# Attention of the first layer: three passes on full-array tiles against plain fp32 on half-array tiles

## The chip, the cores and the metric

The kernel runs on one core of a Trainium2 chip. The metric is the device time of one execution in microseconds (us); the figure quoted for a kernel is the median of its runs. The core has TensorE (PE; its weight loads are PEld), VectorE (DVE), ScalarE (ACT), GpSimd (POOL) and SyncE (SP), each working through its own queue in order.

## The reference, cut to what matters

Four layers work on 128 context tokens and 512 latent tokens, 1024 features each. Layer 0's token mixer is attention with 16 query heads and 4 key/value heads of 64 features: the context tokens attend to themselves, the latent tokens to a band of three blocks of 128 keys around their own block and to 128 cached context keys. Every head has a sink in its softmax.

```python
q, k, v = split_qkv(h, wqkv)          # latent: q, k rotated by position
s_loc = where(|kpos - qpos| <= 128 and 0 <= kpos < T, q . kb * 64 ** -0.5, -1e30)
s_ctx = q . ck * 64 ** -0.5
p = softmax(concat([s_loc, s_ctx, sink]))
o = p_loc @ vb + p_ctx @ cv           # then o @ wo
x = x + gate * (o @ wo)               # then the gated ConvFFN, and layers 1 to 3
```

## The kernel before

Features lie on the partitions and all 640 tokens on the free axis. A projection of full precision is made in three passes: weights and activations are split into a high part (a rounding to fp32r) and a low part (the rest), and `mm3` adds high x high, high x low and low x high. A weight tile of 128 outputs takes 48 matmuls of 320 columns (eight k steps, two halves, three passes). `Weights` loads the tiles in order of their use and splits them (`pump1`: the high part on ScalarE, the low one on VectorE or GpSimd). How far ahead it may go is set by `slots` and `cap`. `Ada` works out the modulation vectors of later layers in quarters of a row block (`micro`) as fillers, on VectorE or on GpSimd followed by a sum on ScalarE. `filler(rate)` gives four quarters times the rate.

The order on every engine is the order in which the program is written; nothing reorders it. In layer 0's mixer the projections come in the order k0, k1, q0, v0, v1, q1 to q7, the first three as a leading group. Attention then goes through 40 units of two heads each: a prompt unit has 128 keys, a latent unit 384 or 512. Query heads are kept in pairs (e = 0 and 1, on partitions 0 to 63 and 64 to 127). Keys of one e are kept with the other 64 partitions zero, so that a score uses the full array. The stages of a unit are

- `scores`: three passes of q x k per head into a PSUM pair, a bf16 mask added by a product with the identity, then on VectorE the maximum over keys (L777) and the bias (L779);
- `exps`: the sink's difference (L784), two exponentials on ScalarE out of PSUM (L786), the sink's exponential (L788);
- `scale`: sum, reciprocal and division of P by it, one head on VectorE (L795), one on GpSimd (L796);
- `transp`: P's blocks of 128 keys transposed on TensorE (L805);
- `evac_hi`, `evac_lo`: P out of PSUM, high part on ScalarE (L811), low part on VectorE (L817);
- `pv`: three passes with V for both heads (L450 to L452 by `mm3`), and every second unit a split of the result into the input of the output projection.

They are a pipeline over units: step u holds the scores and exponentials of unit u, the scaling of u - 1, transposes and copies of u - 2 and the V products of u - 3. Units 0 to 2 are called from `post` of the last query tiles, the others from a loop. The output projection's eight tiles follow (two of them begin during the last steps).

## Time and profile before

| | us |
|---|---|
| median of 3 runs | 2775.72 |
| lowest to highest | 2769.52 to 2777.26 |
| span of the profiled execution | 2775.9 |

The profiled execution lies at the median. TensorE's busy time includes modelled ends of matmuls, which overlap the next one; the pace of a stream is read from the distance between starts. The stages of the first mixer are read from the start: projections, units, output projection.

### The profile page before, as it was taken

Reading aid. Unit: us, or ns where it says so; the run is one execution under the profiler, and the core shown is the slowest. Engines: PE = TensorE matmul, PEld = TensorE weight load, DVE = VectorE, ACT = ScalarE, POOL = GpSimd, SP = SyncE. Lnnn points to the kernel's source line nnn. Section 1 sums busy time; section 2 is a strip of 40 time slices with the busy share of each in tenths; the row PEclk is TensorE's granted clock in tenths of the full one; section 3 lists DMA queues with packets and bytes.
Section 4 is the critical chain, followed back from the end, with each engine's and each line's share of the span. In section 5 each row is a group of like instructions: output and inputs, shape, how many; then the busy total and the mean of one; then the engine's idle time right before and its main releaser. Section 6 shows DMA issues by size and latency. Waiting matters only on the chain.

```text
span 2775.9 us, 45101 instructions
## 1 busy us (share of the span) xinstructions
PE 2706.1 (97%) x18494; PEld 2655.7 (96%) x18494; DVE 1873.1 (67%) x2851; ACT 1097.3 (40%) x1832; POOL 976.9 (35%) x517
## 2 busy tenths in 40 slices
PE   8888999999999999999999999999999999999998
PEld 6776999999999999999999999999999999999998
DVE  5889888695964459586886435968778649534344
ACT  4467454343433235333444222533434425323232
POOL 1555154453620027344542001644354215212121
PEclk9999999999999999999999999999999999999999
DMA  6311434343422225343432222434343124222221
GB/s 245 103 31 39 145 108 135 131 145 129 147 74 70 84 62 171 121 141 118 157 102 74 84 76 70 152 116 151 112 153 135 46 69 138 75 78 69 84 70 45
DMA packets 87489, 295.34 MB, mean 106 GB/s; under 512 B 9585, under 2 KB 15345, under 8 KB 87281
## 3 DMA queue, kind: packets, MB, share of 16 engines
q1 hardware_dynamic: 86706, 292.19, 31.8%
q8 instruction: 146, 2.39, 0.3%
q14 instruction: 61, 0.50, 0.1%
q10 hardware_dynamic: 576, 0.26, 0.0%
HBM read 289.53 MB, written 2.88 MB: 105 GB/s over the span
## 4 chain that ended last, share of the span: by engine, by line
PE 85%; DVE 8%; issue 4%; ACT 1%; POOL 1%; DMA 0%; SPq 0%; POOLq 0%; DVEq 0%; ACTq 0%
PE up L452 15%; PE up L450 15%; PE up L451 15%; PE dn L452 6%; PE dn L450 6%; PE dn L451 6%; PE sc L451 2%; PE sc L452 2%; PE sc L450 2%; DVE t L378 1%; DVE asm L777 1%; DVE asm L784 1%; PE sv L450 1%; PE sv L451 1%; PE sv L452 1%
## 5 line engine op out<-in xcount | busy, mean ns | idle before, releaser
L451 PE MATMUL up<-h,w 128*128 128x320 f32 x2816 | 872.6, 310 | 1.7 <-DVE h L390 1.7
L450 PE MATMUL up<-h,w 128*128 128x320 f32 x2816 | 873.5, 310 | 0.0
L452 PE MATMUL up<-h,w 128*128 128x320 f32 x2816 | 872.1, 310 | 0.0
L86 DVE TENSOR_TENSOR w<-raw,w 128x1024 fp32r<-128x1024 f32 (+1 forms) x269 | 476.4, 1773 | 102.0 <-ACT w L85 94.6
L451 PEld LDWEIGHTS up<-h,w 128*128 128x128 f32 x2816 | 530.4, 188 | 3.1 <-DVE h L390 2.8
L450 PEld LDWEIGHTS up<-h,w 128*128 128x128 f32 x2816 | 530.4, 188 | 0.3
L452 PEld LDWEIGHTS up<-h,w 128*128 128x128 f32 x2816 | 530.4, 188 | 0.0
L212 POOL TENSOR_TENSOR adaq<-adaq,cb 128x1024 f32<-128x1024 f32 x145 | 366.4, 2527 | 370.5 <-ACT adaq L213 321.5
L86 POOL TENSOR_TENSOR w<-raw,w 128x1024 fp32r<-128x1024 f32 (+1 forms) x87 | 211.6, 2433 | 761.8 <-ACT w L85 635.2
L85 ACT CAST w<-raw 128x1024 fp32r<-128x1024 f32 (+1 forms) x356 | 363.3, 1022 | 242.8 <-PE dn L452 163.0
L450 PE MATMUL dn<-g,w 128*128 128x320 f32 x1408 | 436.4, 310 | 0.0
L451 PE MATMUL dn<-g,w 128*128 128x320 f32 x1408 | 435.1, 309 | 0.0
L452 PE MATMUL dn<-g,w 128*128 128x320 f32 x1408 | 435.1, 309 | 0.0
L573 ACT ACTIVATE c<-up,fcv 128x640 f32<-128x640 f32 x176 | 139.9, 795 | 607.9 <-PE up L452 604.0
L575 DVE SCALAR_TENSOR_TENSOR c<-up,fcv,c 128x127 f32<-128x127 f32 x352 | 191.4, 544 | 213.4 <-ACT c L573 213.4
L207 DVE CUSTOM_DVE_ANT_0 adaq<-adaq,cb 128x1024 f32<-128x1024 f32 x145 | 272.6, 1880 | 0.1
L542 DVE SCALAR_TENSOR_TENSOR x<-dn,mod,x 128x128 f32<-128x128 f32 (+3 forms) x204 | 99.4, 527 | 251.0 <-PE dn L452 250.9
L451 PEld LDWEIGHTS dn<-g,w 128*128 128x128 f32 x1408 | 264.3, 188 | 0.3
L450 PEld LDWEIGHTS dn<-g,w 128*128 128x128 f32 x1408 | 264.3, 188 | 0.3
L452 PEld LDWEIGHTS dn<-g,w 128*128 128x128 f32 x1408 | 264.3, 188 | 0.0
L597 POOL TENSOR_TENSOR c<-c,c 128x640 f32<-128x640 f32 x64 | 154.4, 2412 | 158.4 <-DVE c L577 158.4
L577 DVE SCALAR_TENSOR_TENSOR c<-up,fcv,c 128x127 f32<-128x127 f32 x352 | 193.6, 550 | 12.4
(234 smaller groups left out, 4371.5 us busy)
## 6 DMA issues: line engine op xcount, KB each, us to landing
raw<-up SPq DMA_DIRECT2D x176, 512.0 KB, 4.3
adaq<-ada_t SPq DMA_DIRECT2D x145, 512.0 KB, 3.6
raw<-down SPq DMA_DIRECT2D x64, 448.0 KB, 3.5
raw<-down SPq DMA_DIRECT2D x32, 512.0 KB, 3.9
ada<-ada_t SPq DMA_DIRECT2D x31, 512.0 KB, 3.5
raw<-sc_in SPq DMA_DIRECT2D x24, 512.0 KB, 3.5
ada<-ada SPq DMA_DIRECT2D x16, 512.0 KB, 10.2
raw<-sgu_in SPq DMA_DIRECT2D x16, 512.0 KB, 3.5
```

The costliest lines, as they stand in the source:

```text
L85: nc.scalar.copy(w[:, 0, :n], raw[:, :n])
L86: (nc.gpsimd if pool else nc.vector).tensor_tensor(out=w[:, 1, :n], in0=raw[:, :n], in1=w[:, 0, :n], op=ALU.subtract)
L207: nc.vector.tensor_tensor_reduce(out=p0, in0=t, in1=g.cb[:, 0], scale=1.0, scalar=0.0, op0=ALU.mult, op1=ALU.add, accum_out=acc[:, 0:1])
L212: nc.gpsimd.tensor_tensor(out=p1, in0=t, in1=g.cb[:, 1], op=ALU.mult)
L450: nc.tensor.matmul(out, wh, rh, start=first, stop=False)
L451: nc.tensor.matmul(out, wh, rl, start=False, stop=False)
L452: nc.tensor.matmul(out, wl, rh, start=False, stop=last)
L542: nc.vector.scalar_tensor_tensor(out=g.x[:, m, a:b], in0=ps[:, PC0 + a:PC0 + b], scalar=gate[:, m, v:v + 1], in1=g.x[:, m, a:b], op0=ALU.m ...
L573: nc.scalar.activation(c, ps[:, PC0:PC0 + NT], AF.Copy, scale=fc[:, col + 1:col + 2])
L575: nc.vector.scalar_tensor_tensor(out=c[:, a + 1:b], in0=ps[:, PC0 + a:PC0 + b - 1], scalar=fc[:, col:col + 1], in1=c[:, a + 1:b], op0=ALU. ...
L577: nc.vector.scalar_tensor_tensor(out=c[:, a:b - 1], in0=ps[:, PC0 + a + 1:PC0 + b], scalar=fc[:, col + 2:col + 3], in1=c[:, a:b - 1], op0= ...
L597: eng.tensor_tensor(out=cg, in0=cg, in1=c, op=ALU.mult)
```

## The change

- Scores: one plain fp32 product per head on 64 partitions (half of the array's rows), the two heads of a pair on the two halves. Q, K and P are no longer split, K is not padded with zeros, the cached keys go by DMA straight to their place.
- Mask, scale and maximum: one VectorE pass per head (`tensor_tensor_reduce`) adds a row of the bf16 mask strip, scales by -0.125, keeps the running minimum with the sink and writes P. The exponential then reads P from SBUF and sums the sink in as one more key, which GpSimd puts there.
- A latent unit is a pair of heads (e = 0, 1) of one j. A prompt unit has eight heads, so 34 units are left. V products: one fp32 call per head and block onto 64 output partitions (half of the array's columns). The O split comes once for four units.
- The projections are ordered k0, v0, q0 to q3, then k1, v1, q4 to q7. The second six are called from a generator inside units 0 to 20, five k steps a unit; then the first half of the depth of five output tiles (`wo_first`) inside the later units, four k steps a unit. Weights are split one tile ahead there. After the units, the second half of the depth of these five tiles, then the last three tiles.
- The modulation's filler has a rate of 0.5 in place of 0.25 in the units. The rope table sits in one of the four raw buffers in place of a weight buffer.

```diff
-    rope = g.wp.tile([128, 1024], F32, tag="w", name="rope")
+    V, A, PE, G = nc.vector, nc.scalar, nc.tensor, nc.gpsimd
+    rope = g.raw.tile([128, 1024], F32, tag="raw", name="rope")
...
-        at.kst = kst = g.quad.tile([128, 4, 2, NT], F32R, tag="quad", name="kst")
-        at.vst = vst = g.quad.tile([128, 6, 2, 384], F32R, tag="quad", name="vst")
+        kv = g.quad.tile([128, 5120], F32, tag="quad", name="kv")
+        at.kst = kv[:, 0:1280].rearrange("p (a b) -> p a b", a=2)
+        at.kP = kv[:, 1280:1536].rearrange("p (a b) -> p a b", a=2)
+        at.vst = kv[:, 1536:3072].rearrange("p (c a b) -> p c a b", c=6, a=2)
+        at.PT = [kv[:, 3072 + i * 1024:4096 + i * 1024] for i in range(2)]
+        at.O = {0: g.quad.tile([128, 4, 2, NT], F32R, tag="quad", name="O0")}
+        at.strip = g.one.tile([128, 768], BF16, tag="acc", name="strip")
+        V.memset(at.strip, 0.0)
+        V.tensor_copy(at.strip[:, 128:256], mraw[:, 0:128])
+        V.tensor_copy(at.strip[:, 512:640], mraw[:, 128:256])
...
-                unit(u)
-            rope_S(at.qst[:, j, 128:640], ps, t, f"q{j}")
+            rope_S([(at.qst[:, j, 128:640], 0, 512)], t, f"q{j}")
-                A.copy(at.kP[r, 2 * j + e, :], t[r, :128])
-            rope_S(k2[:, :512], ps, t, f"k{j}")
-                    split_to(g, at.kst[r, 2 * j + e, 0, d:d + 256], at.kst[r, 2 * j + e, 1, d:d + 256], k2[r, s:s + 256])
+            A.copy(at.kP[:, j], t[:, :128])
+            rope_S([(at.kst[:, j, 0:256], 0, 256), (at.kst[:, j, 384:640], 256, 512)], t, f"k{j}")
-                v_split(0, 5, j, pt[:, :640].rearrange("p (c d) -> p c d", c=5))
+                A.copy(at.vst[:, 0:5, j, :], pt[:, :640].rearrange("p (c d) -> p c d", c=5))
...
+    KC = {0: (0, 384), 1: (0, 512), 2: (128, 512), 3: (256, 384)}
+    VB = {0: [1, 2, 5], 1: [1, 2, 5, 3], 2: [2, 5, 3, 4], 3: [5, 3, 4]}
+    MO = {0: 384, 1: 128, 2: 128, 3: 0}
+    lat = [(n, j) for n in range(4) for j in range(4)]
+    units = [(0, n, j) for n, j in [(-1, 0)] + lat] + [(1, n, j) for n, j in lat + [(-1, 0)]]
+    def scores(u):
+        gp, n, j = units[u]
+        Pt = g.wp.tile([128, 1058], F32, tag="w", name=f"P{u}")
+        P, sm = Pt[:, :1026].rearrange("p (e k) -> p e k", e=2), Pt[:, 1026:]
+        ps = new_pair(g, f"S{u}")
+        if n < 0:
+            for i in range(4):
+                for e in range(2):
+                    r = slice(64 * e, 64 * e + 64)
+                    PE.matmul(ps[:, e * 512 + i * 128:e * 512 + (i + 1) * 128], at.qst[r, gp * 4 + i, 0:128], at.kP[r, gp, :],
+                              start=i == 0, stop=i == 3)
+        else:
+            kc, nk = KC[n]
+            G.tensor_copy(P[:, :, nk:nk + 1], g.nsink[:, gp * 8:gp * 8 + 8].rearrange("p (e j) -> p e j", e=2)[:, :, j:j + 1])
+            for e in range(2):
+                r = slice(64 * e, 64 * e + 64)
+                PE.matmul(ps[:, e * 512:e * 512 + nk], at.qst[r, gp * 4 + j, 128 + n * 128:256 + n * 128], at.kst[r, gp, kc:kc + nk],
+                          start=True, stop=True)
+        st[u] = (P, ps, sm)
...
+    def soft(u):
+        gp, n, j = units[u]
+        P, ps, sm = st[u]
+        if n < 0:
+            mx, nm, sn, ss, es, ri = (sm[:, 8 * a:8 * a + 8] for a in (0, 0, 1, 2, 1, 3))
+            V.tensor_reduce(out=mx, in_=ps.rearrange("p (h k) -> p h k", h=8), axis=AX.X, op=ALU.max)
+            V.scalar_tensor_tensor(out=nm, in0=mx, scalar=-0.125, in1=g.nsink[:, gp * 8:gp * 8 + 8], op0=ALU.mult, op1=ALU.min)
+            V.tensor_tensor(out=sn, in0=nm, in1=g.nsink[:, gp * 8:gp * 8 + 8], op=ALU.subtract)
+            for h in range(8):
+                A.activation(P[:, h // 4, (h % 4) * 128:(h % 4 + 1) * 128], ps[:, h * 128:(h + 1) * 128], AF.Exp,
+                             bias=nm[:, h:h + 1], scale=0.125, accum_out=ss[:, h:h + 1])
+            A.activation(es, sn, AF.Exp)
+            V.tensor_tensor(out=ss, in0=ss, in1=es, op=ALU.add)
             return
-        n, gp, i, e = units[u]
-        if n >= 0 and i == 0 and e == 0:
-            q2 = g.raw.tile([128, 2, 4, 128], F32R, tag="raw", name=f"qs{u}")
-            split_to(g, q2[:, 0], q2[:, 1], at.qst[:, gp * 4:gp * 4 + 4, 128 + n * 128:256 + n * 128])
-            qs[(n, gp)] = q2
...
     def exps(u):
+        gp, n, j = units[u]
+        P, ps, sm = st[u]
+        if n >= 0:
+            nk = KC[n][1] + 1
+            for e in range(2):
+                A.activation(P[:, e, :nk], P[:, e, :nk], AF.Exp, bias=sm[:, e:e + 1], scale=-1.0, accum_out=sm[:, 2 + e:3 + e])
     def scale(u):
+        gp, n, j = units[u]
+        P, ps, sm = st[u]
+        if n < 0:
+            V.reciprocal(sm[:, 24:32], sm[:, 16:24])
+            for e in range(2):
+                p = P[:, e, :512].rearrange("p (h k) -> p h k", h=4)
+                (V, G)[e].tensor_tensor(out=p, in0=p, in1=sm[:, 24 + 4 * e:28 + 4 * e][:, :, None].to_broadcast([128, 4, 128]), op=ALU.mult)
+            return
+        nk = KC[n][1]
+        V.reciprocal(sm[:, 4:6], sm[:, 2:4])
+        V.tensor_scalar(out=P[:, 0, :nk], in0=P[:, 0, :nk], scalar1=sm[:, 4:5], scalar2=None, op0=ALU.mult)
+        G.tensor_tensor(out=P[:, 1, :nk], in0=P[:, 1, :nk], in1=sm[:, 5:6].to_broadcast([128, nk]), op=ALU.mult)
...
     def pv(u):
+        gp, n, j = units[u]
         pt = st.pop(u)
+        if j == 0:
             ops[0] = g.pb.tile([128, 512], F32, tag="b1", name=f"O{u}")
         ps = ops[0]
+        if n < 0:
+            for e in range(2):
+                PE.matmul(ps[64 * e:64 * e + 64, :], at.vst[:, 0, gp, 64 * e:64 * e + 64], pt[:, e * 512:(e + 1) * 512], start=True, stop=True)
+        else:
+            nb = len(VB[n])
+            for b, c in enumerate(VB[n]):
+                for e in range(2):
+                    PE.matmul(ps[64 * e:64 * e + 64, j * 128:(j + 1) * 128], at.vst[:, c, gp, 64 * e:64 * e + 64],
+                              pt[:, (2 * b + e) * 128:(2 * b + e + 1) * 128], start=b == 0, stop=b == nb - 1)
+        if n < 0 or j == 3:
             c0 = 0 if n < 0 else 128 + n * 128
...
+    def mm_items(ps, w, rhs, nk):
+        for half in (0, 1):
+            for k in range(nk):
+                pe_half(g, ps, w, rhs, half, nk, [k])
+                yield
+    def qkv_rest():
+        for m in range(6, 12):
+            w, ps = g.W.take(), new_pair(g, f"qkv{m}")
+            yield from mm_items(ps, w, norm.rhs, KT)
+            post(m, ps, None)
+            g.W.pump1(True)
+        turns()
+    def orhs(gp):
+        return lambda k, lo, hi: (at.O[gp][:, k, 0, lo:hi], at.O[gp][:, k, 1, lo:hi])
+    WA = KT - 3
+    def wo_first():
+        add = residual(g, 0, 2)
+        for m in range(WA):
+            w, ps = g.W.take(), new_pair(g, f"woa{m}")
+            yield from mm_items(ps, w, orhs(0), 4)
+            if m == 0:
+                g.ada.need(0, 2)
+            add(m, ps, None)
+            g.W.pump1(True)
...
+    g.W.cap = g.W.used + 7
+    proj(g, "qkv", 6, norm.rhs, post, lead=3, plan=plan, hook=hook, rate=1.0, quiet=1)
+    g.W.slots = 1
+    g.W.cap = g.W.used + 6
+    N0 = NU // 2
+    gens = [qkv_rest(), wo_first()]
     def unit(u):
+        gen, n = (gens[0], 5) if u < N0 + 4 else (gens[1], 4)
+        if u < NU:
+            if u == N0 + 3:
+                for _ in gens[0]:
+                    pass
+                g.W.cap = len(g.W.chunks)
+                at.O[1] = g.quad.tile([128, 4, 2, NT], F32R, tag="quad", name="O1")
+            scores(u)
+        if 0 <= u - 1 < NU:
+            scale(u - 1)
+        if u < NU:
+            soft(u)
+        run(gen, n // 2)
+        if 0 <= u - 2 < NU:
+            transp(u - 2)
+        osp()
+        if 0 <= u - 2 < NU:
+            evac(u - 2)
+        if u < NU:
+            exps(u)
+        run(gen, n - n // 2)
+        if u >= 3:
+            pv(u - 3)
+    for u in range(NU + 3):
         unit(u)
-            g.W.cap = len(g.W.chunks)
-        g.W.pump1()
-    out_proj(g, "wo", 0, orhs, nxt, pre=pre)
+        g.ada.filler(0.5)
+    osp()
+    for _ in gens[1]:
+        pass
+    g.W.cap = len(g.W.chunks)
+    g.W.slots = 5
+    g.wpool = False
+    g.W.pump()
+    proj(g, "wob", WA, orhs(1), residual(g, 0, 2, nxt), nk=4, rate=g.rate)
+    proj(g, "wo", 3, lambda k, lo, hi: orhs(k // 4)(k % 4, lo, hi), residual(g, 0, 2, nxt), m0=WA, tail=3, norm=nxt, rate=0.0)
```

## Rows read from the trace of the kernel before

**Rows 1.** The page: the line of the engines (busy us, share of the span, instructions) and the chain that ended last by engine.

```profile
PE 2706.1 (97%) x18494; PEld 2655.7 (96%) x18494; DVE 1873.1 (67%) x2851; ACT 1097.3 (40%) x1832; POOL 976.9 (35%) x517
...
PE 85%; DVE 8%; issue 4%; ACT 1%; POOL 1%; DMA 0%; SPq 0%; POOLq 0%; DVEq 0%; ACTq 0%
```

**Rows 2.** Busy time by stretch of the first mixer: the stretch in us from the span's start, its length, busy us and instructions of each engine, the granted clock of TensorE as a share of full speed, DMA share, GB/s.

```profile
27.50:57.50 30.00, 28.41 (x283) 24.51 (x275) 19.14 (x55) 11.78 (x26) 6.64 (x8) 1.00 0.55 212
57.50:83.20 25.70, 23.47 (x149) 23.20 (x149) 20.52 (x33) 12.17 (x26) 11.17 (x5) 0.93 0.30 92
83.20:144.40 61.20, 48.01 (x312) 47.35 (x313) 46.55 (x91) 25.20 (x77) 35.09 (x22) 0.94 0.31 92
144.40:307.50 163.10, 141.91 (x952) 117.98 (x951) 149.92 (x305) 119.29 (x334) 87.02 (x75) 0.96 0.16 49
307.50:358.00 50.50, 50.50 (x347) 50.34 (x346) 38.86 (x89) 14.40 (x22) 3.27 (x2) 1.00 0.45 140
```

**Rows 3.** Timeline of TensorE over one unit with 512 keys: start, length, engine, line, operation, tiles, shape, count; the first row of each part of the unit, and the first of the next unit.

```profile
183.69 0.40 PE L771 MATMUL S<-kst,qs 128*128 128x512 f32 x1
...
185.39 1.04 PE L805 MATMUL T<-ident,P 128*128 128x128 f32 x8
186.19 0.36 PE L450 MATMUL O<-PT,vst 128*128 128x256 f32 x1
...
187.85 0.40 PE L771 MATMUL S<-kst,qs 128*128 128x512 f32 x1
```

**Rows 4.** The same view over one unit with 384 keys.

```profile
217.59 0.34 PE L771 MATMUL S<-kst,qs 128*128 128x384 f32 x1
...
218.93 0.88 PE L805 MATMUL T<-ident,P 128*128 128x128 f32 x6
219.56 0.36 PE L450 MATMUL O<-PT,vst 128*128 128x256 f32 x1
...
220.94 0.34 PE L771 MATMUL S<-kst,qs 128*128 128x384 f32 x1
```

**Rows 5.** Timeline of TensorE: two runs of plain fp32 products on the full array, the prompt's scores and a product of the Fourier layer. The length is that of the whole run of records.

```profile
227.66 0.61 PE L767 MATMUL S<-kP,qst 128*128 128x128 f32 x4
...
2196.45 1.97 PE L1056 MATMUL fp<-fm,h 128*128 128x256 f32 x8
```

**Rows 6.** Groups of instructions by line and shape: count, busy us, mean ns of one record. The same products, and those of the first modulation on column tiles.

```profile
L248 PE MATMUL adaps<-ada,cstat 128*32 128x128 f32 x256 | 11.4, 313 | 5.2 <-DMA ada<-ada 4.8 <-ACT rbc L356 0.4
...
L767 PE MATMUL S<-kP,qst 128*128 128x128 f32 x32 | 4.9, 274 | 0.0
...
L1056 PE MATMUL fp<-fm,h 128*128 128x256 f32 x16 | 4.6, 404 | 1.4 <-ACT h L382 1.4
```

**Rows 7.** Timeline of TensorE around one burst on column tiles (128*32 is rows by columns of the array in use).

```profile
32.95 0.31 PE L452 MATMUL qkv<-h,w 128*128 128x320 f32 x1
33.19 0.65 PE L248 MATMUL adaps<-ada,cstat 128*32 128x128 f32 x16
33.76 0.42 PE L450 MATMUL qkv<-h,w 128*128 128x320 f32 x1
34.01 0.31 PE L451 MATMUL qkv<-h,w 128*128 128x320 f32 x1
```

**Rows 8.** Groups of instructions of ScalarE up to 360 us, by line and shape.

```profile
L85 ACT CAST w<-raw 128x1024 fp32r<-128x1024 f32 x24 | 24.8, 1038 | 4.0 <-PE qkv L452 3.0 <-PE wo L452 0.8 <-PE O L452 0.2
L144 ACT ACTIVATE ada<-ada 128x512 f32<-128x512 f32 x36 | 22.4, 622 | 26.6 <-POOL ada L143 26.6
L786 ACT ACTIVATE P<-S,asm 128x512 f32<-128x512 f32 x32 | 21.7, 684 | 6.3 <-DVE asm L793 6.1
L786 ACT ACTIVATE P<-S,asm 128x384 f32<-128x384 f32 x32 | 18.3, 577 | 6.9 <-DVE asm L793 6.4 <-DVE asm L779 0.5
L811 ACT CAST PT<-T 128x1024 fp32r<-128x1024 f32 x16 | 16.2, 1011 | 1.2 <-PE T L805 1.0
L786 ACT ACTIVATION_READ_ACCUMULATOR P<-S,asm 128x1 f32 x80 | 15.8, 198 | 0.0
...
L144 ACT ACTIVATION_READ_ACCUMULATOR ada<-ada 128x1 f32 x36 | 6.8, 188 | 0.0
...
L705 ACT COPY q<-qkv 128x512 f32<-128x512 f32 x8 | 4.6, 573 | 7.6 <-PE qkv L452 7.6
...
L706 ACT COPY qst<-qkv 128x128 f32<-128x128 f32 x8 | 2.1, 266 | 0.0
```

**Rows 9.** The same for VectorE.

```profile
L784 DVE TENSOR_TENSOR asm<-vec,asm 128x2 f32<-128x2 f32 x40 | 30.3, 757 | 0.0
...
L777 DVE TENSOR_REDUCE asm<-S 128x2 f32<-128x1024 f32 x16 | 19.4, 1213 | 3.9 <-PE S L775 3.9
L817 DVE TENSOR_TENSOR PT<-T,PT 128x1024 fp32r<-128x1024 f32 x16 | 19.4, 1211 | 0.0
...
L146 DVE CUSTOM_DVE_ANT_0 ada<-ada,cb 128x512 f32<-128x512 f32 x12 | 8.3, 690 | 0.3
```

**Rows 10.** The same for GpSimd.

```profile
L143 POOL TENSOR_TENSOR ada<-ada,cb 128x512 f32<-128x512 f32 x36 | 54.1, 1511 | 17.2 <-DVE part L146 9.7 <-issue 7.5
L86 POOL TENSOR_TENSOR w<-raw,w 128x1024 fp32r<-128x1024 f32 x10 | 24.7, 2477 | 49.9 <-ACT w L85 49.9
...
L796 POOL TENSOR_TENSOR P<-P,asm 128x512 f32<-128x512 f32 x16 | 20.0, 1249 | 26.8 <-PE O L452 15.4 <-DVE asm L794 10.4 <-ACT PT L811 0.9
```

More of the change, by code (lines that the diff above doesn't have):

```diff
@@ L678, in v_split @@
-    def v_split(c0, c1, gp, src):
-        for hl in range(2):
-            for e in range(2):
-                dst = at.vst[:, c0:c1, hl, gp * 192 + e * 128:gp * 192 + e * 128 + 64]
-                s = src[:, :, e * 64:(e + 1) * 64]
-                if hl == 0:
-                    A.copy(dst, s)
-                else:
-                    V.tensor_tensor(out=dst, in0=s, in1=at.vst[:, c0:c1, 0, gp * 192 + e * 128:gp * 192 + e * 128 + 64], op=ALU.subtract)
+        nc.sync.dma_start(out=at.kst[:, :, 256:384], in_=io["cache_k"])
@@ L688, in attention, with rope_S @@
+        nc.sync.dma_start(out=at.vst[:, 5], in_=io["cache_v"].rearrange("p (a b) -> p a b", a=2))
     swap = list(range(16, 32)) + list(range(16))
-    def rope_S(dst, ps, t, nm):
+    def rope_S(dsts, t, nm):
         sh = g.tmp.tile([128, 640], F32, tag="tmp", name=f"sh{nm}")
@@ L694, in rope_S, with turns @@
         V.tensor_tensor(out=t[:, 128:640], in0=t[:, 128:640], in1=cos, op=ALU.mult)
-        V.tensor_tensor(out=dst, in0=t[:, 128:640], in1=sh[:, :512], op=ALU.add)
-    order = ["k0", "k1", "q0", "v0", "v1"] + [f"q{j}" for j in range(1, 8)]
+        for d, a, b in dsts:
+            V.tensor_tensor(out=d, in0=t[:, 128 + a:128 + b], in1=sh[:, a:b], op=ALU.add)
+    order = ["k0", "v0", "q0", "q1", "q2", "q3", "k1", "v1", "q4", "q5", "q6", "q7"]
+    def turns():
+        while at.turn:
+            at.turn.pop(0)()
     def post(m, ps, half):
         kind, j = order[m][0], int(order[m][1:])
-        while at.turn:
-            at.turn.pop(0)()
+        turns()
         if kind == "q":
@@ L799, in transp @@
     def transp(u):
-        n = units[u][0]
-        P = st[u]
+        gp, n, j = units[u]
+        P = st[u][0]
         ps = new_pair(g, f"T{u}")
-        for b in range(len(VB[n])):
-            for gg in range(2):
-                PE.transpose(ps[:, b * 256 + gg * 128:b * 256 + (gg + 1) * 128], P[:, gg, b * 128:(b + 1) * 128], g.ident)
-        st[u] = ps
-    def evac_hi(u):
-        w = len(VB[units[u][0]]) * 256
-        t = g.wp.tile([128, 2, 1024], F32R, tag="w", name=f"PT{u}")
-        A.copy(t[:, 0, :w], st[u][:, :w])
-        st[u] = (t, st[u])
@@ L814, in evac_lo @@
-    def evac_lo(u):
-        w = len(VB[units[u][0]]) * 256
-        t, ps = st[u]
-        V.tensor_tensor(out=t[:, 1, :w], in0=ps[:, :w], in1=t[:, 0, :w], op=ALU.subtract)
+        if n < 0:
+            for h in range(8):
+                PE.transpose(ps[:, h * 128:(h + 1) * 128], P[:, h // 4, (h % 4) * 128:(h % 4 + 1) * 128], g.ident)
+        else:
+            for b in range(len(VB[n])):
+                for e in range(2):
+                    PE.transpose(ps[:, (2 * b + e) * 128:(2 * b + e + 1) * 128], P[:, e, b * 128:(b + 1) * 128], g.ident)
@@ L818, in evac_lo, with evac @@
+        st[u] = ps
+    def evac(u):
+        n = units[u][1]
+        w = 1024 if n < 0 else len(VB[n]) * 256
+        t = at.PT[u % 2]
+        A.copy(t[:, :w], st.pop(u)[:, :w])
         st[u] = t
     def pv(u):
-        n, gp, i, e = units[u]
+        gp, n, j = units[u]
         pt = st.pop(u)
-        if e == 0:
+        if j == 0:
             ops[0] = g.pb.tile([128, 512], F32, tag="b1", name=f"O{u}")
         ps = ops[0]
-        nb = len(VB[n])
-        vo = gp * 192 + e * 64
-        for b, c in enumerate(VB[n]):
-            mm3(nc, ps[:, :256], at.vst[:, c, 0, vo:vo + 128], at.vst[:, c, 1, vo:vo + 128],
-                pt[:, 0, b * 256:(b + 1) * 256], pt[:, 1, b * 256:(b + 1) * 256], b == 0 and e == 0, b == nb - 1 and e == 1)
@@ L840, in osp @@
             dl.pop(0)()
-    dl = []
-    g.W.cap = g.W.used + 12
     def hook(half, k):
@@ L847, in hook, with run @@
             prologue()
-    RQ, RA = 1.0, 0.25
+    def mm_items(ps, w, rhs, nk):
[9 more added lines that the diff above has]
+            g.W.pump1(True)
+        turns()
+    def orhs(gp):
[10 more added lines that the diff above has]
+            g.W.pump1(True)
+    def run(gen, n):
+        for _ in range(n):
+            if next(gen, 1) == 1:
+                return
     g.wpool = True
@@ L881, in attention @@
-    pre = []
-    g.wpool = True
-    proj(g, "qkv", 12, norm.rhs, post, lead=3, plan=plan, hook=hook, rate=RQ, quiet=1)
-    O = [g.quad.tile([128, 4, 2, NT], F32R, tag="quad", name=f"O{q}") for q in range(2)]
-    def orhs(k, lo, hi):
-        return O[k // 4][:, k % 4, 0, lo:hi], O[k // 4][:, k % 4, 1, lo:hi]
-    g.wpool = False
-    for u in range(3, NU + 3):
+    g.W.cap = g.W.used + 7
+    proj(g, "qkv", 6, norm.rhs, post, lead=3, plan=plan, hook=hook, rate=1.0, quiet=1)
+    g.W.slots = 1
@@ L1304, in _layout @@
     sink = i["attn_sink"][0]
-    heads = [(2 * gp + e) * 4 + 2 * ii + gg for gp in range(2) for ii in range(2) for e in range(2) for gg in range(2)]
+    heads = [(2 * gp + e) * 4 + j for gp in range(2) for e in range(2) for j in range(4)]
     o["vec"] = np.ascontiguousarray(np.concatenate([
```

139 lines of the change are left out of this document (18 added, 121 removed).

## The prediction, made before the change was run

> **What bounds the kernel now.** I read the page's engine lines first: TensorE is busy 97% of a span of 2775.9 us and carries 85% of the chain that ended last [rows 1]. So what counts is TensorE time and the moments when TensorE waits. The median of the runs is 2775.72 us, the profiled span 2775.9: the sum below is made against the latter, and no correction is needed. About 0.3% (8 us) is what a measurement of this kernel can tell from no change.
>
> The change touches layer 0's token mixer alone, so next comes the busy time by stage [rows 2]. The mixer's five stretches run from 27.5 to 358.0, 330.5 us: three leading projection tiles (with the first modulation between them) to 57.5; three more tiles to 83.2; six more, with the first three units in between, to 144.4; the other 37 units to 307.5; the output projection to 358. In the last stretch 347 matmuls take 50.5 us with no idle time: 0.146 us for one of 320 columns. In the third, TensorE is idle 13 us of 61, in the fourth 21 of 163, where VectorE is busy 92% of the time. The granted clock is 0.94 to 0.96 there: it falls to its lower level, 1.2 GHz, in pieces after stalls. That costs about 0.06 x 61 + 0.04 x 163 = 10 us.
>
> Then the timeline of one regular unit of 512 keys: TensorE runs without a gap. From 183.69 to 185.39 the score passes and masks take 1.70 us, to 186.19 eight transposes 0.80, to 187.85 the twelve products with V 1.66: 4.16 in all [rows 3]. A unit of 384 keys takes 1.34 + 0.63 + 1.38 = 3.35 [rows 4]. There are 16 of each: 120 us. Thus TensorE itself, not VectorE, sets most units; VectorE's share shows as scattered stalls.
>
> **The change, part by part: TensorE.** Three single passes over zero-padded keys become one plain fp32 product on 64 rows, for two heads side by side. The price of plain fp32 stands in the rows: a call is recorded as two matmuls, and eight records of 256 columns take 1.97 us; less the 0.404 us that one record lasts, over seven steps, that is 0.224 each. Four of 128 take 0.61; less 0.274, over three steps, 0.112 each [rows 5, 6]. Both lie on 0.43 to 0.44 us for 512 columns, so a call costs 0.87. Alone, two heads would take 1.74, as much as the 1.70 they take now. The gain hangs on two half-array calls running at once. No row of before shows a half tile, but a nearer relative is there: the first modulation's products on column tiles of 32. Sixteen such records, fp32 with 128 columns, take 0.65 us, less the 0.27 of one record [rows 6], in place of 16 x 0.112 = 1.8 [rows 7]. Four tiles do run together. I take full overlap for two: 0.87 for a 512 unit's scores, 0.65 for 384; the other end is none, 1.74 and 1.31.
>
> The same rows give the price of changing the tile shape. From the end of the 320-column stream before the burst (32.95 + 0.146) to the point where the next stream has its usual pace (34.01 less 0.146) 0.77 us pass; four groups of 0.109 are 0.44 of them, so going in and out costs 0.33, or 0.17 for each change [rows 7]. The new unit has three changes (scores, back to full array, V products): 0.5 us, 17 us over 34 units. The Trainium skill (TensorEngine Tiling (Array Packing), Key Properties) says that changing the tiling mode drains TensorE; the trace agrees, with 0.33 us for a pair, and this speaks against half tiles in short pieces. The Trainium skill (FP8 and Floating Point Precision, TensorE Precision Notes) counts four passes for true fp32; against the three of before that is a loss of a third per head, unless the heads overlap, and the 0.224 us for 256 columns agrees with it.
>
> V products: per block of 128 keys two calls of 128 columns on two column tiles, 0.22 us if they overlap (0.45 if not), four or three blocks: 0.87 or 0.65. Transposes stay, 0.80 and 0.63. A unit is then 0.87 + 0.80 + 0.87 + 0.5 = 3.04 (512) or 0.65 + 0.63 + 0.65 + 0.5 = 2.43 (384): 16 x 5.47 = 87.5 in place of 120. Two prompt units of eight heads take about 3.1 each. The mask products are gone. V's transposes stay at 0.6 a tile.
>
> **The other engines in a 512 unit.** VectorE loses the low half of P (1.21), the maximum (1.21) and the odd 128x2 addition that averages 0.76 us; it gains two fused passes (scale, mask, running minimum), which I price by the nearest kind, the dot products of the modulation, 0.69 each [rows 9]. The K and Q splits go too. VectorE falls to roughly 100 to 125 us in the unit stretch and no longer sets it. ScalarE: two exponentials (0.684 + 0.198 each), the P copy 1.01 and two modulation sums (0.622 + 0.188 each, two a unit in place of one): 4.4 us; a 384 unit about 3.9 [rows 8]. 16 x (4.4 + 3.9) is 133; the two prompt units, with eight exponentials each, add 15, the copies out of the projections, weight casts and O copies some 21: an estimate of 169 us. GpSimd: two modulation products a unit (1.51 each), P's scaling 1.25 (less for 384 keys), weights 2.48 each [rows 10]: 68 x 1.5 + 34 x 1.1 + 5 x 2.5 and some small pieces, an estimate of 160 us. So both come close to TensorE, and their waits on each other will show.
>
> **The projections between the units.** Six tiles (48 matmuls each, 42 us) go among units 0 to 20; five half-depth output tiles (24 each, 17.5 us) among units 21 to 31. TensorE's work in the unit stretch is 87.5 + 6.2 + 0.6 + 42 + 17.5 = 154 us. These matmuls fill waits, but they bring one. With one slot of look-ahead, the split of the next weight tile is issued only behind the finished tile's copies, just ahead of the first matmul that needs it. For a Q tile: copies 0.57 + 0.27, cast 1.04 [rows 8], the low half on GpSimd 2.48 [rows 10], 4.3 us in which TensorE has nothing queued but the product that waits. Behind it wait the unit's transposes, and ScalarE's P copy behind these. Five boundaries of this kind: 21.5 us. Nothing hides it in program order; the lower bound is 1.9 each, if GpSimd's half came free. The half-depth tiles have 512-wide casts that wait for no copy: 3 us together.
>
> Other waits in the stretch: the last unit is the prompt's, with eight exponentials of 0.57 in a row, and nothing is left to fill the chain of scores, maximum, exponentials, scaling, transposes, copy and products: about 13 us with 3 us of TensorE work, 10 idle. For the ScalarE and GpSimd coupling (GpSimd also waits for each modulation row block, as its raw buffers now share with the rope table) I take 12 us, half of the present 21, since VectorE's part in it goes; bounds 0 and 35 (ScalarE at 169 us plus the boundaries). Clock after stalls: 10 us as now, since the boundary stalls are as long as present ones.
>
> Sum: the first six tiles as now, ending at 83.5. Units: 154 + 21.5 + 3 + 10 + 12 + 10 = 210.5, to 294. Then 264 output matmuls at 0.146 are 38.5, the last unit's split ahead of them 1.5, the norm's products 1.5: to 335.5. The splitting of the output tiles adds five residual adds on VectorE, which is idle then. The prologue's memsets and casts cost nothing now and give nothing back: TensorE's projections cover them. Against 358.0 that is 22.5 us less: 2775.9 - 22.5 = 2753.
>
> **Rivals.**
> - *Half tiles do not overlap.* Scores and V products then cost 1.74 + 1.74 (512) and 1.31 + 1.31 (384): 16 x 3.05 = 49 us more, 52 with the prompts. Some 12 hide under the coupling waits, so 40 remain: 2793, slower. The point from which this decides: under about 55% of the overlap gained, the whole gain is gone. For it: no row shows two tiles, nor row tiles. Against: four column tiles run at once [rows 7]. The Trainium skill (TensorE: Matmul & The Clock Gate, Measured speedup vs the span model) gives 3.07 for four row tiles, an estimate of 77%; then scores would take about 7 us more over all units, which is inside the range.
> - *ScalarE and GpSimd set the pace.* 169 us of ScalarE plus the stalls that it shares with TensorE, with GpSimd waiting for its modulation rows: a stretch of 230 in place of 210, 2773, no change. For it: the doubled modulation rate puts 68 products on GpSimd [rows 10]; against: most of them have a unit's time of slack.
> - *The boundaries hide and TensorE alone sets the end.* 154 + 10 for the end + 7 for the clock = 171: 2714, faster. For it: units that now run without gaps [rows 3]; against: the program order of split and use.
>
> **How the numbers follow.** The forecast's case (2735 to 2767) gets 0.48, the faster one 0.18, ScalarE and GpSimd 0.19 (2767 to 2785), no overlap 0.15 (2785 to 2800). Faster by over 0.3% means below 2767: 0.48 + 0.18 + 0.02 of the third, 0.68. Within 0.3%, 2767 to 2784: 0.16. Slower: 0.16. The range leaves out the upper part of the no-overlap case and the far end of the faster one: 2723 to 2787.
>
> **What would show it.** Right: pairs of score records starting within a few hundredths of a us of each other and a 512-column pair in 0.9 us; about 0.5 us of tile changes a unit; at five tile boundaries a TensorE wait of 2 to 5 us ended by ScalarE's copy or GpSimd's low half; the output projection's end near 335. Wrong: score records one behind the other at 0.43 us; TensorE idle in every unit behind ScalarE; or boundaries without waits.

## The result, and the profile after the change

The changed kernel takes 2806.22 us (median, 2799.6 to 2807.32); the kernel before, on the same chip, 2773.72. The ratio is 1.0118 [1.0101, 1.0134]: slower by 1.2%, where 2753 and faster was forecast, and outside the range of 2723 to 2787. The profiled execution has a span of 2804.2 us, 28.3 more than before; the first mixer ends at 384.7 in place of 358.0, so 26.7 of the 28.3 arise in it.

The page after, as [rows 1]: the engines' busy time, and the chain that ended last by engine.

```profile
PE 2698.7 (96%) x18430; PEld 2627.0 (94%) x18430; DVE 1802.6 (64%) x2712; ACT 1092.6 (39%) x1793; POOL 999.2 (36%) x560
...
PE 82%; issue 8%; DVE 4%; POOL 3%; ACT 3%; DMA 0%; SPq 0%; ACTq 0%; POOLq 0%; DVEq 0%
```

VectorE has 70 us less to do and TensorE 7 less, yet "issue", time in which an engine waited for nothing that the profile shows, has doubled on the chain. Now the mixer by stretch, in the columns of [rows 2]: three projection tiles, three more, units 0 to 33 in two halves with the second six projections and the first output halves between them, and the rest of the output projection.

```profile
27.50:57.50 30.00, 29.23 (x274) 25.52 (x274) 20.76 (x59) 13.65 (x30) 0.00 (x0) 0.94 0.52 198
57.50:81.00 23.50, 21.73 (x149) 21.62 (x149) 20.16 (x32) 8.31 (x19) 13.95 (x8) 1.00 0.41 127
81.00:204.00 123.00, 91.60 (x609) 68.63 (x607) 60.98 (x123) 65.86 (x173) 71.62 (x69) 0.85 0.16 53
204.00:324.00 120.00, 93.97 (x663) 71.61 (x663) 70.19 (x145) 74.80 (x200) 76.97 (x76) 0.86 0.19 60
324.00:384.70 60.70, 47.10 (x272) 46.12 (x273) 35.47 (x77) 14.95 (x24) 3.26 (x2) 0.86 0.34 112
```

The first six tiles end at 81.0 (83.5 forecast). The units take 243 us (210.5 forecast), the output projection 60.7 (41.5). TensorE is busy 76% of the units' time, ScalarE 58%, GpSimd 61%: no engine is full. And the granted clock is 0.85 to 0.86 over 304 us, where it was 0.94 to 1.00 [rows 2].

The arithmetic itself is as fast as hoped. The timeline of TensorE in a stretch without waits:

```profile
141.31 1.13 PE L731 MATMUL S<-kv,qst 64*128 64x512 f32 x4
142.37 0.42 PE L450 MATMUL qkv<-h,w 128*128 128x320 f32 x1
...
146.66 1.13 PE L731 MATMUL S<-kv,qst 64*128 64x512 f32 x4
```

Four score records of 512 columns on half the rows take 1.06 us to the next stream's start. From one pair of scores to the next, 5.35 us, lie fifteen projection matmuls (2.2 us at 0.146) and a unit: 3.16, forecast 3.04.

So the loss lies in waits and in the clock. TensorE's own waits in the mixer (sum, count, longest, in us):

```profile
PE qkv L450 <- ACT w L85: 20.2, 5, 6.7
PE wo L450 <- DVE x L542: 10.5, 2, 7.4
PE qkv L452 <- POOL w L86: 8.8, 5, 2.0
PE woa L450 <- ACT w L85: 6.3, 5, 1.6
PE woa L452 <- POOL w L86: 5.0, 4, 2.7
PE wob L451 <- DVE O L551: 3.1, 1, 3.1
...
PE woa L452 <- DVE w L86: 2.1, 1, 2.1
```

One of the five boundaries between projection tiles (here behind V's), in the timeline of all engines:

```profile
119.24 1.27 POOL L143 TENSOR_TENSOR adap<-ada,cb 128x512 f32<-128x512 f32 x1 [10.68 <-DMA ada<-ada_t]
120.58 1.28 POOL L143 TENSOR_TENSOR ada<-ada,cb 128x512 f32<-128x512 f32 x1
121.81 0.19 POOL L728 COPY P<-vec 128x2 f32<-128x2 f32 x1
122.03 0.75 DVE L751 CUSTOM_DVE_ANT_0 P<-S,strip,vec 128x512 f32<-128x512 f32 x1 [5.75 <-POOL P L728]
...
127.16 0.67 ACT L697 COPY v<-qkv 128x640 f32<-128x640 f32 x1
...
128.25 1.04 ACT L85 CAST w<-raw 128x1024 fp32r<-128x1024 f32 x1 [0.41 <-ACT v L697]
129.34 0.63 PE L450 MATMUL qkv<-h,w 128*128 128x320 f32 x1 [5.62 <-ACT w L85]
...
131.78 0.64 PE L452 MATMUL qkv<-h,w 128*128 128x320 f32 x1 [1.53 <-POOL w L86]
132.21 0.47 PE L450 MATMUL qkv<-h,w 128*128 128x320 f32 x1
132.48 0.47 PE L451 MATMUL qkv<-h,w 128*128 128x320 f32 x1
```

Read it from the top. GpSimd waited 10.68 us for a modulation row block. Behind its two products in GpSimd's queue stands the copy of the sink into P, 0.19 us long; VectorE's mask pass waited 5.75 for it. ScalarE's exponentials of that unit and of the next came late, the last at 126.44; only then did ScalarE copy the finished V tile and cast the next weight, for which TensorE waited 5.62, and 1.53 more for GpSimd's half. Then matmuls follow each other at 0.27 us, not 0.146: the lower level, 1.2 GHz, lasts until about 137. The boundary was forecast; the sink copy's delay was not, and the slow stretches were put at 10 us in all.

The row block came late because it was asked for late: SyncE issued its load at 115.58, right after ScalarE's last sum over the block before (to 115.56). Amid the units SyncE waits 47.9 us for such sums ahead of these loads; weights, row blocks and the rope table share four raw buffers. GpSimd waits 29.1 us for row blocks in the units here and 29.2 in e11 below, and not at all in e5 and e13, which have no projections between the units. No run gives the blocks a buffer more, so what this alone is worth stays open.

In the output projection it is VectorE (timeline):

```profile
351.77 0.69 DVE L146 CUSTOM_DVE_ANT_0 junk<-ada,cb 128x512 bf16<-128x512 f32 x1 [3.39 <-DMA ada<-ada_t]
...
353.12 1.00 DVE L542 SCALAR_TENSOR_TENSOR x<-wob,mod,x 128x128 f32<-128x128 f32 x2
```

The residual add, which frees TensorE's accumulator, stands behind modulation row blocks that arrive one DMA at a time.

### The profile page after: what moved, and what is told of

It reads as the page before. It is cut to its first block, busy times and chain, and to the rows that moved or that the text cites. A ratio compares the mean times of both kernels' runs of the same rounds, so it can differ in the third digit from the quotient of the medians.

```text
span 2804.2 us, 44749 instructions
## 1 busy us (share of the span) xinstructions
PE 2698.7 (96%) x18430; PEld 2627.0 (94%) x18430; DVE 1802.6 (64%) x2712; ACT 1092.6 (39%) x1793; POOL 999.2 (36%) x560
## 4 chain that ended last, share of the span: by engine, by line
PE 82%; issue 8%; DVE 4%; POOL 3%; ACT 3%; DMA 0%; SPq 0%; ACTq 0%; POOLq 0%; DVEq 0%
PE up L450 15%; PE up L452 15%; PE up L451 15%; PE dn L451 6%; PE dn L452 6%; PE dn L450 6%; PE sc L450 2%; PE sc L452 2%; PE sc L451 2%; POOL w L86 1%; DVE t L378 1%; PE qkv L450 1%; PE qkv L452 1%; ACT P L761 1%; PE qkv L451 1%
## 5 line engine op out<-in xcount | busy, mean ns | idle before, releaser
L451 PE MATMUL up<-h,w 128*128 128x320 f32 x2816 | 872.6, 310 | 1.7 <-DVE h L390 1.7
L86 DVE TENSOR_TENSOR w<-raw,w 128x1024 fp32r<-128x1024 f32 (+2 forms) x269 | 474.4, 1767 | 99.6 <-ACT w L85 91.6
L451 PEld LDWEIGHTS up<-h,w 128*128 128x128 f32 x2816 | 530.5, 188 | 3.1 <-DVE h L390 2.8
L86 POOL TENSOR_TENSOR w<-raw,w 128x1024 fp32r<-128x1024 f32 (+2 forms) x92 | 217.4, 2365 | 772.0 <-ACT w L85 645.3
L85 ACT CAST w<-raw 128x1024 fp32r<-128x1024 f32 (+2 forms) x361 | 363.8, 1011 | 239.9 <-PE dn L452 163.2
L451 PE MATMUL dn<-g,w 128*128 128x320 f32 x1408 | 435.0, 309 | 0.0
L451 PEld LDWEIGHTS dn<-g,w 128*128 128x128 f32 x1408 | 264.3, 188 | 0.3
```

The source lines that it names most:

```text
L85: nc.scalar.copy(w[:, 0, :n], raw[:, :n])
L86: (nc.gpsimd if pool else nc.vector).tensor_tensor(out=w[:, 1, :n], in0=raw[:, :n], in1=w[:, 0, :n], op=ALU.subtract)
L451: nc.tensor.matmul(out, wh, rl, start=False, stop=False)
```

## Experiments

**Theory after the first reading.** Four causes add up: the weight split issued only at a tile's end (*boundary*), the sink copy in GpSimd's queue (*sink*), modulation on VectorE ahead of residual adds (*tail*), and a lower clock behind each stall. **Rival:** the placing cannot pay at all, since TensorE has no holes to fill in regular units; or the half tiles are worth little. All ratios are against the kernel before; after's is 1.0118.

Read the times together with the end of the first mixer, where all the edits lie. Here is the profiled execution of each kernel: us to the first matmul behind the mixer, and from there to the end.

| | mixer ends | the rest |
|---|---|---|
| before | 358.0 | 2417.9 |
| after | 384.7 | 2419.5 |
| e1, e2, e3 | 379.3, 378.8, 379.0 | 2419.3, 2416.5, 2419.6 |
| e8, e4 | 355.9, 350.2 | 2421.2, 2412.0 |
| e6, e7 | 359.1, 365.5 | 2420.1, 2419.4 |
| e5, e13 | 315.4, 327.5 | 2412.0, 2419.3 |
| e10, e11 | 326.1, 337.3 | 2411.8, 2413.5 |
| e9, e12 | 315.4, 363.7 | 2412.4, 2420.6 |

In the rest TensorE does the same work in all of them and waits as long (14.6 to 14.8 us), yet it takes from 2411.8 to 2421.2: behind some of these waits the granted clock falls in one execution and not in another (35.5 us at the lower level in e8, 15.1 in e5). So up to 9 us between two times can have nothing to do with the edit; the end of the mixer, from one execution each, is the other half of the reading.

### Three causes, one at a time

```diff
 # e1_early_split (likewise in wo_first, item 2 of 8; and a cap of used + 7 for used + 6)
-            yield from mm_items(ps, w, norm.rhs, KT)
+            for i, _ in enumerate(mm_items(ps, w, norm.rhs, KT)):
+                if i == KT:
+                    g.W.pump1(True)
+                yield
             post(m, ps, None)
-            g.W.pump1(True)
 # e2_sink_vector
-            G.tensor_copy(P[:, :, nk:nk + 1], g.nsink[:, gp * 8:gp * 8 + 8].rearrange("p (e j) -> p e j", e=2)[:, :, j:j + 1])
+            V.tensor_copy(P[:, :, nk:nk + 1], g.nsink[:, gp * 8:gp * 8 + 8].rearrange("p (e j) -> p e j", e=2)[:, :, j:j + 1])
 # e3_tail_modulation, ahead of the output projection: loads run two blocks ahead
+    g.ada.pool = "half"
+    g.ada.ahead = 1
+    g.ada.load()
```

> The split of the next weight tile is issued in the middle of the running tile in place of behind its last copy; nothing else. Theory A (the waits at the tile boundaries and the low clock behind them make the loss): the 29 us of TensorE waits at the query boundaries and the 13 at the half-depth tiles fall to under 8, and the low-clock time in the unit stretch halves, which gives back some 20 more: 2806 - 55 = about 2750. Theory B (GpSimd, with the sink copy queued behind the modulation products at the doubled rate, sets the pace): the waits move to the scores and the exponentials, 2806 - 20 = about 2786.

> The sink's value is written into P by VectorE in place of GpSimd; nothing else. Theory A: VectorE's and ScalarE's waits for GpSimd's small copy (17 and 8 us) lie beside the boundary waits and give back nothing: 2800 to 2806. Theory B: they lie on the path: 2806 - 18 = about 2788.

> In the output projection the modulation rows left over are loaded two ahead and half of their products go to GpSimd; nothing else. If the 10.5 us that TensorE waits for VectorE's residual adds there come from VectorE waiting for one row block at a time, they vanish, with 2 to 4 us of low clock: about 2793. If they come from VectorE's own work (residual adds, weight halves), no more than 4 us come back: about 2802.

Measured: e1 2799.28 us, 1.0087 [1.0070, 1.0104]; e2 2798.35, 1.0081 [1.0066, 1.0096]; e3 2800.17, 1.0089 [1.0074, 1.0104]. Each gives only 6 to 8 us (5.4 to 5.9 at the mixer's end). VectorE's wait for the sink copy in the changed kernel, and the waits in e1 (all engines, then TensorE), say why:

```profile
DVE P L751 <- POOL P L728: 17.0, 8, 6.0
```

```profile
DVE P L751 <- POOL P L728: 67.8, 23, 9.6
...
PE T L787 <- DVE P L751: 14.5, 8, 3.9
PE qkv L450 <- DVE P L751: 13.3, 3, 5.8
```

The waits for the weight are gone, but VectorE now waits 67.8 us for the sink copy, against 17.0 in the changed kernel: the boundary had hidden it. In e2 the sink copy is out of the way and the boundaries remain, beside 10.4 us for GpSimd's half:

```profile
PE qkv L450 <- ACT w L85: 15.8, 5, 4.3
```

### Causes together

e8_early_and_sink is e1 and e2 in one; e4_all adds e3.

> Early split and sink on VectorE, without the tail's edit. If each wait takes the place of the other, so that only both edits together give time back: 2806 - 34 = about 2772. If the edits only add up (7 and 8 us alone): about 2791.

> The three edits together. Theory A: 2806 - 55 - 3 - 13 = about 2735, faster than the kernel before by about 1.3%. Theory B: 2806 - 20 - 18 - 13 = 2755. If the parts hide each other, above 2765.

Measured: e8 2777.7 us, 1.0013 [1.0002, 1.0025]: 28 less than the changed kernel, where the two gave 15 alone (at the mixer's end 28.8 and 11.3). e4 2766.21, 0.9973 [0.9956, 0.9990]: 40 less, where all three alone gave 21 (34.5 and 17.0). The waits stood side by side, and each took the other's place. The tail's edit is worth 6 us of the mixer alone, and 6 beside the other two: of the 12 between the times of e8 and e4, the rest lies behind the mixer. The mixer of e4 ends at 350.2, against 358.0 and 384.7; TensorE's largest wait is now for the other product in GpSimd's queue, the second head's scaling:

```profile
PE T L788 <- POOL P L776: 15.4, 9, 3.2
```

### The scaling off GpSimd

```diff
 # e6_scale_vector: e4 and
-        G.tensor_tensor(out=P[:, 1, :nk], in0=P[:, 1, :nk], in1=sm[:, 5:6].to_broadcast([128, nk]), op=ALU.mult)
+        V.tensor_scalar(out=P[:, 1, :nk], in0=P[:, 1, :nk], scalar1=sm[:, 5:6], scalar2=None, op0=ALU.mult)
```

> The three edits of the fourth experiment, and P's scaling of the second head on VectorE too. The fourth left 15 us of TensorE waits for GpSimd's scaling, queued behind the modulation products. Theory B (GpSimd's queue is what is left): 2766 - 12 = about 2754. If the waits go to ScalarE's copy or VectorE's pass instead: 2762 or more.

Measured: 2778.67 us, 1.0009 [0.9996, 1.0023]: 12 slower than e4 (8.9 at the mixer's end). That wait went, others came, of which the largest two:

```profile
PE T L788 <- DVE P L752: 10.8, 6, 3.3
PE S L732 <- ACT kv L795: 7.2, 3, 2.7
```

So that queue was not the cause by itself; the last section has a likelier one, which no run tests for e6.

### Is the overlap worth what was forecast?

```diff
 # e7_same_half: e4 and
-                r = slice(64 * e, 64 * e + 64)
+                r = slice(0, 64)
```

> The fourth experiment with both heads' scores of a latent unit on the same 64 rows, so that they can't overlap (the scores of the second head are those of the first: the output is not the reference's). It adds 16 x (0.8 + 0.6) = 23 us of TensorE work. If TensorE's time stands on the path in most units: 2766 + 20 = about 2786. If the waits of the other engines absorb it: below 2775.

Measured: 2786.6 us, 1.0046 [1.0031, 1.0061], 20 more than e4 (15.3 at the mixer's end). In its timeline four records of 512 columns last 1.98 us in place of 1.13, and of 384 columns 1.55 (0.92 side by side, in e5 below):

```profile
164.25 1.98 PE L732 MATMUL S<-kv,qst 64*128 64x512 f32 x4
...
170.46 1.55 PE L732 MATMUL S<-kv,qst 64*128 64x384 f32 x4
```

The differences, 0.85 and 0.63 us, times sixteen each are 23.7 us; 15 of them arrive in the mixer. The prediction's first rival, no overlap, is refuted for the scores.

### The arithmetic without the placing

```diff
 # e5_units_alone: all twelve projections first, modulation at the old rate; e3's edit too
-    proj(g, "qkv", 6, norm.rhs, post, lead=3, plan=plan, hook=hook, rate=1.0, quiet=1)
+    proj(g, "qkv", 12, norm.rhs, post, lead=3, plan=plan, hook=hook, rate=1.0, quiet=1)
...
-        run(gen, n // 2)
...
-        run(gen, n - n // 2)
...
-        g.ada.filler(0.5)
+        g.ada.filler(0.25)
...
+    proj(g, "woa", WA, orhs(0), residual(g, 0, 2), nk=4, rate=0.5 * g.rate)
 # e13_units_alone_rate: e5, but
+        g.ada.filler(0.5)
```

> The arithmetic of the change without the projections between the units: all twelve projection tiles ahead of the units, the output projection behind them (with the tail's modulation as in the third experiment), filler rate 0.25 as before. If what failed is the placing of the projections, this gains: TensorE's unit work is 87 in place of 120 us, but a chain of scaling, masked pass and exponentials of about 4.2 us (512 keys) and 3.4 us (384) now sets a unit: 122 us and a 15 us end: 2776 - 15 = about 2760. If TensorE, idle in a quarter of each unit, falls to its lower clock for long, nothing is gained: 2776 or more.

> The fifth experiment (2730) with the filler's rate in the units doubled to that of the change; nothing else. ScalarE's work in a 512 unit rises from 3.6 to 4.4 us and GpSimd's from 2.9 to 4.3, against 3.0 of TensorE: if the rate by itself costs, 37 x 0.8 = 30 us less some 8 saved behind the units, about 2750. If there is room for it: 2722 to 2732.

Measured: e5 2730.18 us, 0.9858 [0.9839, 0.9878], faster than both kernels; e13 2750.0, 0.9920 [0.9906, 0.9935]. Both leave the sink copy on GpSimd. By stretch, in the columns of [rows 2]: e5's units and output projection, and ninety microseconds amid its units; then the same ninety of e13:

```profile
125.00:244.50 119.50, 101.20 (x857) 64.80 (x856) 77.14 (x226) 105.89 (x281) 91.84 (x104) 0.93 0.16 50
244.50:315.30 70.80, 62.12 (x394) 60.90 (x393) 44.74 (x92) 26.41 (x55) 22.90 (x15) 0.93 0.39 122
...
140.00:230.00 90.00, 85.36 (x744) 53.93 (x743) 58.84 (x186) 87.39 (x219) 76.30 (x92) 0.99 0.16 48
```

```profile
140.00:230.00 90.00, 70.39 (x560) 43.12 (x560) 63.98 (x149) 82.73 (x216) 86.59 (x95) 0.94 0.23 71
```

In e5 TensorE is busy 95% of these ninety, ScalarE 97%, and the clock is 0.99: regular units have no holes for projections to fill. (Of the 18 us that are open in the whole stretch, 8.9 and 4.3 are two waits, at its start and at its end.) TensorE's timeline there:

```profile
166.12 1.13 PE L732 MATMUL S<-kv,qst 64*128 64x512 f32 x4
167.18 1.09 PE L788 MATMUL T<-ident,P 128*128 128x128 f32 x8
168.20 1.09 PE L811 MATMUL O<-kv 128*64 128x128 f32 x16
169.23 0.92 PE L732 MATMUL S<-kv,qst 64*128 64x384 f32 x4
```

A unit of 512 keys takes 3.11 us (3.04 forecast, 4.16 in [rows 3]), and the mixer 288 in place of 330.5. With the modulation's rate doubled, e13, GpSimd is busy 96% of the ninety and TensorE 78%, and the units take 145.0 us in place of 119.5. The output projection gives 12.9 back (57.9 us at a clock of 1.00, in place of 70.8 at 0.93: TensorE waits 8.7 us for residual adds there in e5, and not in e13). So the mixer ends 12 us later; the other 7 of the 20 in the time lie behind it.

### Is any of the placing worth it?

e11_q_between has only the six projections between the units, e10_wo_between only the output halves; both with the early split, the sink copy on VectorE and e3's edit, e11 at rate 0.5, e10 at 0.25.

```diff
 # e11
-    gens = [qkv_rest(), wo_first()]
+    gens = [qkv_rest(), iter(())]
 # e10, in e5's order of the projections
+    gens = [iter(()), wo_first()]
```

> The other half of the placing: the last six of the twelve projection tiles between the units (split in the middle of the tile before, sink on VectorE, filler rate 0.5, tail's modulation as in the third), the output projection behind the units. If the query tiles carry the loss of the placing, this lies near the fourth experiment: about 2760. If the output tiles carry it, near the fifth: about 2735.

> The fifth experiment (2730) with one half of the placing put back: the first half of the depth of five output tiles runs between the units (split in the middle of the tile before, sink on VectorE), the query tiles stay ahead of the units. TensorE's idle time in the units of the fifth experiment is 18 us. If matmuls fill it: about 2720. If the placing hurts by the waits that it brings: 2740 or more.

Measured: e11 2752.21 us, 0.9928 [0.9912, 0.9945]; e10 2741.35, 0.9891 [0.9873, 0.9908]. At equal rates, e11 against e13 is +2 in the time but +9.8 at the mixer's end, although e13's VectorE still waits 8.0 us for the sink copy on GpSimd: at rate 0.5 the projections between the units cost some 10 us. The output halves cost 11 (e10 against e5, where the sink's engine differs too) or 14 (e4 against e11); at the mixer's end 11 and 13. e10's largest wait is `PE wo L451 <- DVE x L543`, 14.2 us: the last tiles wait for residual adds.

### The modulation's share

e9_no_unit_modulation is e4 (without the loads two ahead), e12_after_no_modulation the changed kernel, each with most of the units' row blocks left out.

```diff
+    g.ada.queue = q[:p] + [x for x in q[p:24 - 2] if x[2] >= 7] + q[24 - 2:]
...
-        g.ada.filler(0.5)
+        g.ada.flush()
```

> The fourth experiment with the modulation fillers of the units left out: about 16 of the 24 row blocks of layer 0's later modulation vectors are not worked out (their sums stay zero, so the output is not the reference's). If the modulation products on GpSimd and their sums on ScalarE, at the doubled rate, are what the fourth experiment still waits for: 2766 - 25 = about 2741 or less. If it is the alternation of units and projections as such (tile copies, rope and casts in the units' queues): 2755 or more.

> The changed kernel with the modulation fillers of the units left out (some 16 row blocks of layer 0's later modulation vectors are not worked out; the output is not the reference's), with the late split and the sink copy on GpSimd as they are. If GpSimd's and ScalarE's modulation queue alone makes the loss, the boundaries become short and the time falls near the ninth experiment: 2735 to 2745. If the late split keeps its own price (ScalarE's copies and cast, GpSimd's half: 4.3 us at five boundaries, 1.5 to 3 at five more, and low clock behind them): 2760 to 2775.

Measured: e9 2731.18 us, 0.9850 [0.9835, 0.9865], 35 below e4; e12 2786.54, 1.0058 [1.0042, 1.0075], 20 below the changed kernel. Without that work the changed kernel is still slower than before; its boundaries remain, and the granted clock in its units is 0.86, where e9, without boundary waits, has 0.96:

```profile
PE qkv L451 <- ACT w L85: 14.4, 5, 4.4
PE woa L451 <- ACT w L85: 13.1, 2, 12.7
PE qkv L453 <- POOL w L86: 8.7, 5, 1.9
```

The 12.7 us are no boundary's price. The edit leaves two row blocks that are worked off in one go in front of the first residual add, and ScalarE's cast stands behind their eight sums; e9 has the same spot, with one wait of 8.7. So what the work costs in its place is nearer to 33 than to 20 us in the changed kernel (an estimate, 20 + 12.7). And e9, its 8.7 us included, only equals e5, which leaves nothing out.

## Why the prediction was wrong

Right were the parts on the operations. *Overlap of two half tiles*, taken over from the column tiles of [rows 7]: full: e7's two scores on one half take 1.91 us to the next stream's start, on two halves 1.06. *A unit of 3.04*: 3.16, and 3.11 in e5; of the miss, 0.05 is a slip, since 0.224 for 256 columns is 0.448 for 512, not the 0.43 to 0.44 that the sum went on with. *First six tiles*: 81.0. *Boundaries between tiles wait for the cast and GpSimd's low half*: so they do. In e5, which keeps the arithmetic, mends the tail and places nothing between the units, the gain is 1.4%.

Wrong were four terms of the sum; the mixer ended 49 us after the 335.5 forecast. Busy and idle time in the stretches part them. In the units TensorE was busy 185.6 us, where 154 at full clock and 10 for the clock were set; it was idle 57.4, where 46.5 were. In the tail it was busy 47.1 against 40 and idle 13.6 against 1.5. Of the 185.6, by the trace's records of the clock, 49.6 were at the lower level, which costs half of them, some 25; that leaves some 161 at full clock. e9, with the same TensorE work, was busy 162.6, with 7.6 at the lower level: 159. So the misses are 15 and 7 us of the lower clock, 6 of the units' size, 11 and 12 of waits, less 2.5 of the earlier start, good to a few us.

- *"Clock after stalls: 10 us as now, since the boundary stalls are as long as present ones"* failed most: some 25 in the units, and 7 in the tail, where nothing was set. Before, the units ran at 0.94 to 0.96 [rows 2]; now, with stalls of up to 6.7 us at ten boundaries, at 0.85. In e9, where they are gone, the units run at 0.96, in the middle of e5 at 0.99. From the changed kernel to e4, TensorE's idle time in the units falls from 57 to 36 us and its busy time at the lower level from 49.6 to 35.8: 20 us of waits and 7 of clock. The Trainium skill (TensorE: Matmul & The Clock Gate, Loop structure matters more than you think) calls a loop good whose matmuls stay back to back, and bad one with a long wait ahead of each matmul; on the waits the runs agree. Spreading a tile's k steps over the units is not by itself the fault: e9 spreads them as the changed kernel does, at 0.96.
- *"Five boundaries: 21.5"* measured 29.0. Without the modulation in the units (e12) it is 23.1, so the size was right and ScalarE and GpSimd reached the split late. *"The half-depth tiles wait for no copy: 3 us together"* measured 13.4: 7.1 are waits for the low half of the weight, which that term left out. The other waits came to 15 us, where 22 were set.
- *The sink copy*, one of "some small pieces", had no wait in the sum, and of GpSimd's products the text said that "most of them have a unit's time of slack". Its 0.2 us don't count; its place in GpSimd's queue behind products that wait for a DMA does. Yet [rows 10] showed GpSimd's products waiting. The question to ask of a new instruction is what stands ahead of it.
- *"Five residual adds on VectorE, which is idle then"*: it was not. It works off modulation row blocks there, and TensorE waits 10.5 and 3.1 us. e3's edit gives back 6 us.

The second rival, ScalarE and GpSimd set the pace, was right in kind and not in size. The doubled modulation rate costs 25.5 us in the units (e13 against e5), but the changed kernel's GpSimd is only 61% busy: it held up the others by its order, and VectorE's multiplication by its products (last section). And the premise *"these matmuls fill waits"* fails: the largest wait in the units before, 11.2 us of some 34, was for VectorE's low half of P, which the change itself removes. Once it is gone, e5 shows 5% of TensorE's time open in the middle of the units.

What stays open: whether some order with the projections between units and the modulation at rate 0.25 beats e5. At rate 0.5 (e11 and e13) it does not pay. Nor is e5 the end: its output projection takes 12.9 us more than e13's.

## What to carry to other kernels

Before filling an engine's holes, ask whether the rest of the change closes them; here the arithmetic with a mended tail gave 1.4% (44 us), and the changed kernel, with the filling, its doubled side work and an unmended tail, is 76 us slower than that. A short instruction in an in-order queue costs what stands ahead of it; here it was better on the engine that uses its result, although it takes 14.9 us of VectorE there in all (e4). When a repair brings little, look at the waits of the repaired kernel before dropping it: two causes that hide each other gave 15 us apart and 28 together. And compare where the work was changed, not only at the end: behind the mixer the same work took up to 9 us more or less.
